# One step moved inside several side jobs of a hybrid encoder layer: turns, keys, logarithm rounds, buffers and stores

## The chip, the cores and the metric

The kernel runs on one core of one Trainium2 chip. The metric is the device time of one execution in microseconds, the median over several executions. Lower is better.

## The reference, cut to what matters

One layer of an encoder is applied to two groups of rows with the same weights: 1024 rows ("sample") and 256 rows ("prompt"), each 2048 wide, in float32. Everything between the two large products is done per head or per group of heads:

```python
hn = rms_norm(x, norm_g)
xbc, z_ssd, dt_raw, q, k, v, z_att, mq, z_mem = split_cols(hn @ w_in, IN_SIZES)
xbc = silu(centred_dwconv(xbc, conv_w, conv_b))            # 5 taps along the rows
dt = softplus(dt_raw + dt_bias); A = -exp(a_log)
y = ssd_scan(xs, dt[0], A[0], B, C) + reversed(ssd_scan(...)) + d_skip * xs
o_ssd = rms_norm(y * silu(z_ssd))                          # 16 heads of 64, chunks of 128 rows
o_att = window_attention(rms_norm(q), rms_norm(k), v, sink) * silu(z_att)
mk, mv = split_cols(rms_norm(mem) @ w_mem_kv)              # 256 memory rows for each group
pm = softmax(rms_norm(mq) @ rms_norm(mk).T / sqrt(128))    # 4 heads of 128
o_mem = (pm @ mv) * silu(z_mem)
return x + concat([o_ssd, o_att, o_mem]) @ w_out
```

The scan needs running sums of `dt * A` along a chunk (`acs`) and the logarithm of `dt`.

## The kernel before, in words

The 1280 rows make ten tiles of 128 (`NT`), in two groups of five. Tiles 0 to 7 are the sample, 8 and 9 the prompt. Every large product is taken in a split form: a float32 operand is cut into a high and a low part (ScalarE copies the high part, VectorE subtracts it, `wsplit`, L214 to L218), and three matmuls add up high times high, high times low and low times high.

The large products run as blocks, one behind the other, and TensorE does them in program order. `block_tok` (L244) computes 512 columns for up to five row tiles: for each of 16 slices of the inner dimension it loads 256 KB of weights on SyncE (L223), splits them, and issues 15 matmuls. `block_feat` does the same with the result turned. `block_pair` computes two halves at once with seven products in place of eight; 14 such blocks stand near the start and 8 at the end. When a tile of a block is complete, an eviction function takes it from the accumulator to SBUF and stores it to HBM: `ev_gate` (gates z0 and z1), `ev_raw` (queries q and mq), `ev_out` (the output) and others. In the last slice of a block the tiles finish one after the other.

An eviction's buffer comes from a ring. Rings `evt` and `evu` of the pool `ev` have two buffers each. Tiles with an odd number take `evt`, the others `evu`, so that tile 4 of a block takes the buffer that tile 0 had. The ring `ch` of the pool `rp` has four buffers (`CH`) and serves the loads that refill the rows (`fill_direct`, L185), the output's evictions and the sums near the end.

Everything that isn't a large product is a side job, written as a generator, whose parts between two `yield`s are its steps. Two lanes hold the queued jobs: lane 0 the keys (`k_prep`), the window attention (`attn`) and the memory attention (`mem_attn`), lane 1 the preparation of dt (`dt_prep`) and the scan (`ssd_up`, `ssd_down`). Behind each slice of a block, `pump` (L158) adds a rate to what is owed to each lane and runs as many steps, in turns between the lanes; the rates stand in `RATES` (2.25 and 2.5 steps a slice in the second query block, for instance). A job that ends takes one more step, so that a final `yield` is an empty step. `need` runs a lane's steps until a named job is done. The framework then gives each engine one order of instructions, by the order in the program and by its own estimate of when an operand is ready; `tc.high_priority` moves evictions and splits forward. On the chip, each engine goes through its order without overtaking.

The jobs that the change touches:

- `mem_attn(t)` (L773 to L870). Step 1 takes the query (fetched by the job before, `fetch_next`, L524), step 2 the sum of squares, step 3 the split of the query and the load of the gate, step 4 is empty, steps 5 and 6 are the scores of two heads each (`scores`: matmuls L811 to L813, maximum L815, exponentials L821 on ScalarE, the division L827 on VectorE). Steps 7 and 8 are empty, 9 and 10 turn the weights (`turn_`: GpSimd's clearing of one word L654, four transposes L647, copy L839 on ScalarE), 11 and 12 are the values (`values`: matmuls L850, product L853). Step 11 also fetches the next query, step 12 stores the result (L869). Step 13 is the empty end.
- `k_prep(t)` (L530 to L560). Step 3 splits the key, step 4 is empty, step 5 does four transposes (L554), two copies and the fetch of what comes next; step 6 is the empty end.
- `dt_prep(t0)` (L568 to L636), once for each group of five tiles. Step 1 is the softplus (L578 to L589), step 2 the product with A (`da`, L593), step 3 a first value of the logarithm (L596, L597), step 5 a triangular mask on GpSimd (`lower`, L602), step 7 the running sums on TensorE (`pacs`, L608 to L610), their copy on ScalarE, two rounds that refine the logarithm (an exponential L614 on ScalarE, then L616 to L620 on VectorE, a reciprocal among them) and the exponentials of the sums (L621, L622); step 8 turns the sums (`pact`) and stores them. Steps 4 and 6 are empty, step 9 is the empty end.
- `refill_o(grp, when)` (L1531). It is called behind each slice `k` of a block. At the slices named in `when` it first makes sure by `need` that a part of the layer's output is complete, and then queues four loads of that part (L188, one a slice) with their splits (L197 to L201), which follow two slices after the load. In the first output block it is called with `{1: 2, 5: 3}`: the scan's two halves.
- `ev_pair(u)` (L1232). It adds the seven products of one of the last 8 blocks into two row tiles `r0`, `r1` of 2 x 320 (adds on VectorE, L1240) and stores them: all of `r0` behind product 3 (L1256), one half of `r1` behind product 7 (L1259), the other behind product 4, the last (L1262). The products come in the order 1, 2, 6, 5, 3, 7, 4.

## Time and profile before

| what | value |
|---|---|
| median of 3 runs | 1772.34 us (1772.21 to 1774.35) |
| profiled execution | 1773.66 us, of which the span of the core is 1772.0 us |
| TensorE busy | 1762.2 us (99% of the span) |
| VectorE, ScalarE, GpSimd busy | 1246.0, 901.6, 555.6 us |
| data moved by DMA | 301.16 MB, mean 170 GB/s |
| granted TensorE clock | full in all 40 slices of the span |

The profile is of one execution. In the rows that follow, PE is TensorE's matmuls, PEld its weight loads, DVE is VectorE, ACT ScalarE, POOL GpSimd and SP SyncE; a "q" behind the name means the engine's queue, for instance a DMA that SyncE issues. `L827` is line 827 of the kernel. A row in order of time gives the start and the duration in us, engine, line, instruction, the tile written and the tiles read, the shape and how many; in square brackets stand the idle time of that engine just before and what ended it. A row in the list of waits gives the engine and line that waited, what it waited for, the total in us, the number of times and the longest. The end of a matmul is modelled, so starts are safer than ends.

### The profile page before, as it was taken

The numbers are of one execution on the slowest core, as the hardware profiler recorded it, in microseconds if no ns is written. First come the engines' busy times: TensorE is split into PE (matmuls) and PEld (weight loads), VectorE is DVE, ScalarE is ACT, GpSimd is POOL, SyncE is SP. The second block draws the span as 40 slices with busy tenths as digits, with TensorE's granted clock in tenths as the row PEclk, the third lists the DMA queues.
The fourth block names the chain that finished last, engine by engine and source line by source line (L and its number), as shares of the span: only waits on it lengthen the run. The fifth ranks groups of instructions, "written<-read, shape, count | busy, mean of one in ns | idle before, by whom it ended". The sixth has DMA issues, their size and how long they took to land. (4 is left out here: it accounts for less than half of the span.)

```text
span 1772.0 us, 31942 instructions
## 1 busy us (share of the span) xinstructions
PE 1762.2 (99%) x11044; PEld 1608.4 (91%) x11044; DVE 1246.0 (70%) x2351; ACT 901.6 (51%) x2010; POOL 555.6 (31%) x980
## 2 busy tenths in 40 slices
PE   9999999999999999999999999999999999999999
PEld 7889999999998999999889988888988888899999
DVE  5596788888868878878665676566776654766665
ACT  6555455554434756656454555544446533543332
POOL 0105899998810100001001000011110000058775
PEclk9999999999999999999999999999999999999999
DMA  9654444445446645454545645557777755744442
GB/s 308 189 182 130 136 151 146 144 140 169 124 140 209 197 134 151 140 153 122 186 121 173 201 149 161 172 161 249 225 246 226 257 188 148 218 142 148 145 144 77
DMA packets 208210, 301.16 MB, mean 170 GB/s; under 512 B 19568, under 2 KB 86192, under 8 KB 208048
## 3 DMA queue, kind: packets, MB, share of 16 engines
q1 hardware_dynamic: 207904, 299.06, 54.1%
q8 instruction: 87, 1.43, 0.3%
q14 instruction: 75, 0.61, 0.1%
q10 hardware_dynamic: 144, 0.06, 0.0%
HBM read 236.36 MB, written 62.69 MB: 169 GB/s over the span
## 5 line engine op out<-in xcount | busy, mean ns | idle before, releaser
L217 DVE TENSOR_TENSOR wl<-wraw,wh 128x512 fp32r<-128x512 f32 (+1 forms) x480 | 346.4, 724 | 238.4 <-ACT wh L216 225.4
L216 ACT ACTIVATE wh<-wraw 128x512 fp32r<-128x512 f32 (+1 forms) x480 | 292.2, 613 | 301.6 <-PE acc L270 154.6
L268 PE MATMUL acc<-wh,xH 128*128 128x512 f32 (+1 forms) x1088 | 418.1, 385 | 0.0
L270 PE MATMUL acc<-wh,xL 128*128 128x512 f32 (+1 forms) x1088 | 410.4, 377 | 0.0
L269 PE MATMUL acc<-wl,xH 128*128 128x512 f32 (+1 forms) x1088 | 409.5, 376 | 0.0
L270 PEld LDWEIGHTS acc<-wh,xL 128*128 128x128 f32 x1088 | 204.2, 188 | 37.0 <-issue 0.2
L268 PEld LDWEIGHTS acc<-wh,xH 128*128 128x128 f32 x1088 | 204.3, 188 | 36.5 <-issue 2.7
L269 PEld LDWEIGHTS acc<-wl,xH 128*128 128x128 f32 x1088 | 204.5, 188 | 35.0 <-issue 1.2
L303 PE MATMUL acc<-xH,wh 128*128 128x320 f32 x640 | 203.0, 317 | 0.0
L305 PE MATMUL acc<-xH,wl 128*128 128x320 f32 x640 | 198.8, 311 | 0.0
L304 PE MATMUL acc<-xL,wh 128*128 128x320 f32 x640 | 198.5, 310 | 0.0
L216 ACT ACTIVATE sh<-ws 128x384 fp32r<-128x384 f32 x176 | 91.4, 523 | 204.8 <-POOL ws L1284 111.2
L217 DVE TENSOR_TENSOR sl<-ws,sh 128x384 fp32r<-128x384 f32 x176 | 124.4, 710 | 98.3 <-ACT sh L216 96.0
L1284 POOL TENSOR_TENSOR ws<-wraw 128x128 f32<-128x128 f32 x176 | 113.8, 646 | 202.4 <-DMA wraw<-in_w_in_pairs_dram 90.5
L303 PEld LDWEIGHTS acc<-xH,wh 128*128 128x128 f32 x640 | 120.1, 188 | 2.9 <-issue 2.4
L304 PEld LDWEIGHTS acc<-xL,wh 128*128 128x128 f32 x640 | 120.2, 188 | 1.7 <-issue 1.4
L305 PEld LDWEIGHTS acc<-xH,wl 128*128 128x128 f32 x640 | 120.2, 188 | 1.0 <-issue 0.9
L1284 POOL TENSOR_TENSOR ws<-wraw,ws 128x128 f32<-128x128 f32 x176 | 116.5, 662 | 13.8
L1284 POOL TENSOR_TENSOR ws<-ws,wraw 128x128 f32<-128x128 f32 x176 | 118.2, 671 | 0.0
L1284 POOL TENSOR_TENSOR wraw<-wraw 128x128 f32<-128x128 f32 x176 | 111.5, 633 | 13.7
L654 POOL MEMSET lgw<- 128x1 f32 x40 | 4.2, 105 | 312.0 <-DVE lg L718 161.6
L377 DVE SCALAR_TENSOR_TENSOR c<-u,vec,c 128x638 f32<-128x638 f32 (+1 forms) x96 | 90.0, 939 | 1.1 <-ACT c L372 0.4
(442 smaller groups left out, 3931.1 us busy)
## 6 DMA issues: line engine op xcount, KB each, us to landing
wraw<-in_w_in_laid_dram SPq DMA_DIRECT2D x176, 256.0 KB, 2.9
wraw<-in_w_in_pairs_dram SPq DMA_DIRECT2D x112, 256.0 KB, 2.7
wraw<-in_w_out_laid_dram SPq DMA_DIRECT2D x64, 256.0 KB, 3.6
wraw<-in_w_out_pairs_dram SPq DMA_DIRECT2D x64, 256.0 KB, 2.7
rf<-ac SPq DMA_DIRECT2D x40, 256.0 KB, 4.0
rb<-ac SPq DMA_DIRECT2D x40, 256.0 KB, 4.7
wraw<-in_w_mem_laid_dram SPq DMA_DIRECT2D x32, 256.0 KB, 4.3
xst<-in_x_sample_dram SPq DMA_DIRECT2D x20, 256.0 KB, 5.3
```

The costliest lines, as they stand in the source:

```text
L216: a = A.activation(h, raw, AF.Copy)
L217: b = V.tensor_sub(l, raw, h.bitcast(F32))
L268: T.matmul(ps[t][:, :n], sh, h[:, :n], start=(k_ == 0), stop=False)
L269: T.matmul(ps[t][:, :n], sh, l[:, :n], start=False, stop=False)
L270: T.matmul(ps[t][:, :n], sl, h[:, :n], start=False, stop=(k_ == KT - 1))
L303: T.matmul(o, sh, cur["H", q][:, m, c], start=(k == 0), stop=False)
L304: T.matmul(o, sh, cur["L", q][:, m, c], start=False, stop=False)
L305: T.matmul(o, sl, cur["H", q][:, m, c], start=False, stop=(k == KT - 1))
L377: V.scalar_tensor_tensor(out=c[0], in0=u[:, k:k + n], scalar=cw[k], in1=c[0], op0=ALU.mult, op1=ALU.add)
L654: G.memset(w.bitcast(F32)[(slice(None),) + tuple(slice(n - 1, n) for n in shape)], 0.0)
L1284: G.tensor_tensor(out=o, in0=x, in1=y, op=op)
```

## The change

Six edits, each of which moves or splits something; no product is added or removed.

- `out_place` (new): evictions of tiles 3 and 4 in the second group's gate and query blocks (z0, z1, q, mq) take a buffer of the ring `ch`. All others stay.
- `k_prep`: the fetch stays in step 5, the transposes and copies go to step 6, in place of the empty end.
- `dt_prep`: the mask goes to step 2; the running sums go to step 5 with the exponentials of the sums and the first round; the second round is step 6; the rest of step 7 and step 8 stay.
- `mem_attn`: the turns go to steps 10 and 11, the values to 12 and 13; the fetch stays in step 11.
- `ev_pair`: the upper half of `r0` is stored behind product 2, so that behind product 3 only the lower half is left; the add of `w` to `r1` is done in two halves, behind products 6 and 5.
- `refill_o` with `sooner=1` and `{2: 2, 6: 3}` in the first output block: `need` stays at slices 1 and 5, the loads and splits go one slice later.

```diff
+    def out_place(i, base, name):
+        if i > 2 and base == 0 and name == "qs":
+            return fin.tile([P, 512], F32, tag="tH7" if i == 4 else "tL7", name=name)
+        if i > 2 and base:
+            return rp.tile([P, 640], F32, tag="ch", name=name, bufs=CH)[:, :512]
+        return ev.tile([P, 512], F32, tag="evt" if i % 2 else "evu", name=name)
...
     def ev_gate(c, base):
-            z = ev.tile([P, 512], F32, tag="evt" if i % 2 else "evu", name="zs")
+            z = out_place(i, base, "zs")
...
     def ev_raw(dst, base):
-            if base == 0 and i > 2:
-                z = fin.tile([P, 512], F32, tag="tH7" if i == 4 else "tL7", name="qs")
-            else:
-                z = ev.tile([P, 512], F32, tag="evt" if i % 2 else "evu", name="qs")
+            z = out_place(i, base, "qs")
...
     def k_prep(t):
         yield
         yield
+        fetch_next()
+        yield
         ps = psum("pk")
...
         A.activation(kL[:, :, c], hv(ps[:, 256:], 2), AF.Copy)
-        fetch_next()
-        yield
...
     def dt_prep(t0):
         V.tensor_mul(t5(da), dt_all[:, ts, :], aneg.unsqueeze(1).broadcast_to([P, 5, 32]))
+        lower = w2("lower")[:, :P]
+        G.affine_select(out=lower, in_=ones, compare_op=ALU.is_ge, fill=0.0, base=0,
+                        pattern=[[-1, P]], channel_multiplier=1)
         yield
...
-        yield
-        yield
-        lower = w2("lower")[:, :P]
-        G.affine_select(out=lower, in_=ones, compare_op=ALU.is_ge, fill=0.0, base=0,
-                        pattern=[[-1, P]], channel_multiplier=1)
         yield
         yield
         ps = psum("pacs")
...
         A.activation(ac[:, :320], ps[:, :320], AF.Copy)
+        A.activation(flat(eacs_all), ac[:, 0:160], AF.Exp)
+        A.activation(flat(cd_all), ac[:, 160:320], AF.Exp)
         for _ in range(2):
             A.activation(s, l, AF.Exp)
...
             V.scalar_tensor_tensor(out=l, in0=d, scalar=2.0, in1=l, op0=ALU.mult, op1=ALU.add)
-        A.activation(flat(eacs_all), ac[:, 0:160], AF.Exp)
-        A.activation(flat(cd_all), ac[:, 160:320], AF.Exp)
+            yield
         V.tensor_sub(wj, l, ac[:, 0:160])
...
     def mem_attn(t):
         scores(1)
-        yield
-        yield
-        yield
+        for _ in range(4):
+            yield
         turn_(0)
         yield
         turn_(1)
+        fetch_next()
         yield
         values(0)
-        fetch_next()
         yield
         values(1)
         S.dma_start(oT_d[1][grp][:, :, tc_], hv(oT, 4))
-        yield
...
     def ev_pair(u):
             elif p == 2:
                 add(r0[:, 0], ps, r0[:, 0])
+                S.dma_start(y_turned[rows_[0], :320], r0[:, 0])
             elif p == 6:
                 add(w[:, 0], ps, w[:, 0])
+                add(r1[:, 0], w[:, 0], r1[:, 0])
             elif p == 5:
                 add(w[:, 1], ps, w[:, 0])
                 add(r0[:, 1], w[:, 1], r0[:, 1])
-                add(r1, w, r1)
+                add(r1[:, 1], w[:, 1], r1[:, 1])
             elif p == 3:
                 add(r0[:, 1], ps, r0[:, 1])
-                S.dma_start(hv(y_turned[rows_[0], :], 2), r0)
+                S.dma_start(y_turned[rows_[0], 320:], r0[:, 1])
...
-    def refill_o(grp, when):
+    def refill_o(grp, when, sooner=0):
         def f(k):
+            if k + sooner in when:
+                need((attn, mem_attn, ssd_down, ssd_down)[when[k + sooner]], range(grp * 5, grp * 5 + 5))
             if k not in when:
                 return []
             q = when[k]
-            need((attn, mem_attn, ssd_down, ssd_down)[q], range(grp * 5, grp * 5 + 5))
...
-        tok("o", w_out_rows(c), ev_out(c * 512), None if c else refill_o(0, {1: 2, 5: 3}), grp=1)
+        tok("o", w_out_rows(c), ev_out(c * 512), None if c else refill_o(0, {2: 2, 6: 3}, sooner=1), grp=1)
```

## The prediction, on record before the run

> **What bounds the kernel now.** I read the page first, then the busy time by stage, then the list of who waited for whom on TensorE, then the instructions in order of time around each of those waits. Columns of the stage rows: microseconds from and to, length, then busy time and count of matmuls, weight loads, VectorE, ScalarE, GpSimd, then the granted clock.
>
> ```profile
> span 1772.0 us, 31942 instructions
> PE 1762.2 (99%) x11044; PEld 1608.4 (91%) x11044; DVE 1246.0 (70%) x2351; ACT 901.6 (51%) x2010; POOL 555.6 (31%) x980
> ...
> 0.00:490.00 490.00, 488.36 (x2973) 461.67 (x2974) 370.86 (x567) 256.13 (x499) 311.34 (x482) 1.00 0.53 165
> ...
> 812.00:946.00 134.00, 132.06 (x840) 117.95 (x839) 95.09 (x216) 74.53 (x196) 12.51 (x27) 1.00 0.52 158
> ...
> 1182.00:1312.00 130.00, 128.62 (x839) 112.22 (x839) 96.35 (x199) 60.32 (x145) 19.50 (x52) 1.00 0.71 223
> 1312.00:1500.00 188.00, 186.85 (x1001) 155.37 (x1000) 105.91 (x205) 88.33 (x206) 11.15 (x33) 1.00 0.67 212
> ...
> 1592.00:1772.00 180.00, 176.35 (x1202) 176.08 (x1200) 114.77 (x182) 65.45 (x117) 127.40 (x217) 1.00 0.42 128
> ```
>
> TensorE is idle for 1772.0 - 1762.2 = 9.8 us in all, at the full granted clock. 1.6 us of that lie in the first stage and 3.65 us in the last one, nearly all behind the last matmul. The three stages in the middle hold 1.94 + 1.38 + 1.15 = 4.5 us. So this change, which removes no matmul, can take about 4.5 us off the middle and a part of the tail. These are the waits:
>
> ```profile
> ...
> PE pst L937 <- ACT fh L952: 1.1, 1, 1.1
> PE pmt L647 <- DVE mpr L827: 1.1, 1, 1.1
> PE ppt L647 <- ACT pT L734: 1.0, 1, 1.0
> PE pmo L850 <- ACT mpT L839: 0.8, 1, 0.8
> PE pr L647 <- ACT so L1088: 0.4, 1, 0.4
> ...
> ```
>
> Every one is a single event (the two rows left out lie in the first and the last stage). The first four, 1.1 + 1.1 + 1.0 + 0.8 = 4.0 us, are what the edits touch.
>
> **Memory attention turned one step later.** The wait at 846 us:
>
> ```profile
> 845.87 0.62 DVE L827 TENSOR_SCALAR mpr<-mpr,mden 128x256 f32<-128x256 f32 x2
> 846.37 0.54 PE L647 MATMUL pmt<-identr,mprw 128*128 128x128 f32 x4 [1.06 <-DVE mpr L827]
> ...
> 848.54 1.05 PE L850 MATMUL pmo<-mpT,mv 128*128 128x128 f32 x8
> ```
>
> The second turn stands on TensorE before VectorE has divided the weights. The number of steps of one memory attention stays 13, because the empty end step is dropped; scores stay at steps 5 and 6, the turns go from 9 and 10 to 10 and 11, the values from 11 and 12 to 12 and 13, and the fetch of the next query stays in step 11. I call a step place the point behind each group of main matmuls where the lanes' steps are put. The next place here is that of the first values, at 848.54, 3.2 us behind the point where TensorE now begins to wait (846.37 - 1.06): minus 1.06 us. Nothing is late next there, as the values move a place on as well. With the turn go GpSimd's clearing of one word and ScalarE's copy, with the values VectorE's product and the store on SyncE; the fetch was ahead of that store before and stays so.
>
> A later turn has a price where three steps share a place, as in the third memory attention (steps 10, 11, 12 at 875 us). Now it holds turn 1, values 0, values 1; after, turn 0, turn 1, values 0. Its rows, with dt_prep's logarithm beside them:
>
> ```profile
> 874.92 0.46 PE L647 MATMUL pmt<-identr,mprw 128*128 128x128 f32 x4
> 875.91 0.34 ACT L614 ACTIVATE s<-l 128x160 f32<-128x160 f32 x1 [2.05 <-DVE l L620]
> ...
> 876.67 0.58 ACT L839 ACTIVATE mpT<-pmt 128x512 f32<-128x512 f32 x1
> 877.30 1.16 PE L850 MATMUL pmo<-mpT,mv 128*128 128x128 f32 x8 [0.79 <-ACT mpT L839]
> ```
>
> ScalarE stands 2.05 us before the exponential of the second logarithm round, and the copy of the turned weights, ready to go at 874.92 + 0.46 = 875.4, is queued behind it. In the change the two exponentials of the running sums go ahead of the rounds, each round gets a step of its own, and the sums come two steps sooner. I count minus 0.79 for this. In its place stands the new order: the values need a turn (0.46) and a copy (0.58), and beside the copy lie only another turn (0.46) and two transposes of dt_prep, half a turn, so some 0.3 us of the 1.04 since the turn's start stay open. An estimate of plus 0.3 us; the ends are 0 (main matmuls are put in between) and 0.79 (what the place costs now). Behind it are queued all main matmuls.
>
> **The sums of dt_prep two steps sooner.** Step counts again stay (9), but the matmuls that add up the decays go from step 7 to step 5, with ScalarE's copy of them and the two exponentials. At 2.5 steps a place the second dt_prep's steps fall as 1-2, 3-5, 6-7, 8-9, which fits the sums at 871 us (step 7) one place ahead of the turn at 875. So they move to the place of the second scores:
>
> ```profile
> 866.85 0.28 PE L813 MATMUL pms<-mkH,mql 128*128 128x256 f32 x1
> L593 DVE TENSOR_TENSOR e<-dt_all,aneg x2: 319/322/324, 537.1 to 868.6; 128x160 f32<-128x160 f32 x2
> L609 PE MATMUL pacs<-e,lower x4: 275/275/275, 544.4 to 871.0; 128*128 128x80 f32 x4
> ```
>
> Their operand is written on VectorE at 868.6 + 0.3 = 868.9. Put right behind the last score matmul at 866.9, TensorE would wait 2.0 us, with all main matmuls and ScalarE's copy of the sums behind it; put behind main matmuls of the next place, 0. I take 1.0, the size that misplaced steps have in this trace (0.8 to 1.1), and keep 0 and 2.0 as ends. The first dt_prep has no such price: its operand stands at 537.4, its sums run at 544.4, and two steps at 1.7 a place are one or two places of 3.45 us, so not before 537.5. The mask on GpSimd moves three steps forward; GpSimd is busy for 12.5 us of 134 in this stage, so it costs nothing.
>
> **Own places for the fourth and fifth eviction.** The last rows of the query block at 1227 us:
>
> ```profile
> 1227.20 0.60 ACT L341 ACTIVATE qs<-acc 128x512 f32<-128x512 f32 x1 [1.06 <-DMA mq<-qs]
> ...
> 1228.12 0.65 PE L647 MATMUL ppt<-identr,lgw 128*128 128x128 f32 x4 [0.95 <-ACT pT L734]
> DMA to landing us min/median/max: 2.2/3.6/5.4
> ```
>
> The fifth eviction takes the buffer of the first, whose store is still under way; ScalarE stands in front of it, the window attention's copy pT stands behind, TensorE behind that. With a buffer of the ring "ch", which no fill uses during those blocks, the wait of 1.06 goes, and with it TensorE's 0.95. [...]
>
> **Wait for the store ahead of the load.** The chain of waits around 1330 us:
>
> ```profile
> 1317.83 0.23 PE acc L270
> ...
> 1319.97 4.54 DMA oT<-so
> ...
> 1324.90 5.86 DMA chd<-oT
> 1331.52 0.62 ACT wh L216
> ...
> 1334.10 0.64 ACT fh L952
> 1334.78 0.50 PE pst L937
> ```
>
> SyncE waits for the last output to land, then loads it; ScalarE's first split of that load waits for it with a weight split queued behind, and the state's matmuls are late. The change finishes the scan one place earlier than it asks for the load. From place to place lie fifteen matmuls of 0.23, 3.45 us, and the steps, most of the 4.54; loads and splits both go one place on, so that the store has landed when the load's turn comes: minus 1.1 us. The later load brings the splits of a row block from five to four places ahead of its use, over 13 us: no cost.
>
> **Keys.** Their transposes go one step later and the fetch stays in its step. No row of TensorE's waits names them: 0, between minus 0.3 and plus 1.0, the size of one misplaced step.
>
> **The tail.** VectorE sets the end behind the last matmul:
>
> ```profile
> 1765.75 0.49 DVE L1240 TENSOR_TENSOR yu<-acc,yu 128x320 f32<-128x320 f32 x1 [0.39 <-PE acc L1318]
> 1766.27 1.23 DVE L1240 TENSOR_TENSOR yr<-yu,yr 128x320 f32<-128x320 f32 x2
> 1767.82 1.41 DVE L1240 TENSOR_TENSOR yr<-accm,yr 128x640 f32<-128x640 f32 x2
> L1240 DVE TENSOR_TENSOR yr<-yu,yr 128x320 f32<-128x320 f32 x8 | 4.0, 500 | 0.3
> ```
>
> One half of the 640-wide add moves into the idle 0.39 us ahead of 1765.75. It takes 0.50 and so delays the next add by 0.11; the pair of 1.23 becomes two adds of 0.50, 0.23 less. Together minus 0.12 us. 160 of the last 640 KB go out sooner, with one more issue on SyncE, which no engine waits for: an estimate of minus 0.1, between minus 0.3 and plus 0.1. [...]
>
> **Sum.** Minus 1.06 - 0.79 - 0.95 - 1.1 - 0.2, plus 0.3 + 1.0: minus 2.8 us. The profiled execution took 1773.66 us (span 1772.0 and 1.66 around it), so 1770.9 for it; the runs shown have a median of 1772.34, 1.3 lower, and I forecast 1769.5 for the median. About 0.2%, 3.5 us here, is what a measurement of this kernel can tell from no change: the lines are 1768.8 and 1775.9.
>
> **The rivals.**
>
> First, all four waits go and the sums of dt_prep find their operand ready, because main matmuls stand ahead of them: no plus at all, 1772.34 - 4.1 = 1768.2. For it speaks that TensorE meets late steps only five times between 490 and 1500 us, so most are placed well; against it the 2.0 us between 866.9 and 868.9. Chance 0.33.
>
> Second, the waits change their places and do not go: 2.0 us at the sums and 0.79 twice where turns and values share a place give back 3.6 of 4.1: 1771.8. For it speaks that all steps after scores shift and that VectorE, 71% busy in that stage, is late there whatever the order. Chance 0.20.
>
> Third, slower: SyncE holds the weights. The memory attention's store is issued in order, and where it waits, the next weight load waits too:
>
> ```profile
> 1389.77 0.33 SPq L223 DMA_DIRECT2D wraw<-in_w_out_laid_dram  x1
> 1396.66 0.53 SPq L869 DMA_DIRECT2D oT<-moT  x1
> 1398.44 0.40 SPq L223 DMA_DIRECT2D wraw<-in_w_out_laid_dram  x1
> 1412.18 0.63 ACT L216 ACTIVATE wh<-wraw 128x512 fp32r<-128x512 f32 x1 [1.59 <-PE acc L270]
> wraw<-in_w_out_laid_dram SPq DMA_DIRECT2D x64, 256.0 KB, 3.6
> ```
>
> After the change this store waits one place longer, 3.45 us and the steps, about 5 us. The weights that it holds back are needed 1412.18 - 1398.44 = 13.7 us after their issue and land in 3.6, so a margin of 10 us is left, 5 after the change. It decides only from 10 us on; a hold of 18 us would cost 8 us of TensorE and give 1772.34 - 2.8 + 8 = 1777.5. Chance 0.07.
>
> **How the numbers follow.** The forecast's own case has 0.40, with 1768.8 to 1771.3 around it. Faster by over 0.2% is the first rival, 0.33; slower the third, 0.07; within 0.2% the forecast and the second, 0.60. The range goes from 1767.0 (first rival, with the tail's and the keys' lower bounds and some 0.5 us of other waits) to 1772.8 (second rival with one more wait of 1.0).
>
> **What would show it.** In the changed kernel's list of TensorE's waits the rows for pmt, ppt, and pst should be gone, and no eviction should wait for its own store. The sums (pacs) should stand near 867 us; a wait of TensorE for L593's tile there is the 1.0 to 2.0 us that I count. ScalarE should not stand before the second logarithm round with a copy behind it. At the end, two stores of 160 KB should replace the one of 320 KB, and the last add should start about 0.1 us sooner against the last matmul. The prediction is wrong if TensorE's idle time in the middle stages stays near 4.5 us, or if a weight split waits for its load.

## The result, and the profile after

The changed kernel is slower: a median of 1776.50 us (7 runs, 1776.12 to 1781.02) against 1772.51 of the kernel before on the same chip (7 runs, 1771.51 to 1774.43), a ratio of 1.0026 with a 95% interval of 1.0016 to 1.0036. (A ratio, here and below, is estimated from all the runs; the quotient of the two medians differs from it by up to 0.0006.) The forecast was 1769.5 and the range ended at 1772.8. The profiled execution took 1776.12 us, its span 2.4 us more than that of before. From the page of the changed kernel, the span and the busy time:

```profile
span 1774.4 us, 31955 instructions
...
PE 1764.4 (99%) x11044; PEld 1609.0 (91%) x11044; DVE 1250.4 (70%) x2359; ACT 901.5 (51%) x2010; POOL 557.2 (31%) x980
```

The number of matmuls is unchanged, but TensorE is *busy* 2.2 us longer (1764.4 against 1762.2): the lost time is not all idle time. The stage rows (columns as in the prediction) say where:

```profile
490.00:812.00 322.00, 320.74 (x2255) 301.13 (x2254) 248.31 (x546) 180.52 (x438) 31.72 (x77) 1.00 0.51 157
812.00:946.00 134.00, 131.97 (x837) 117.57 (x837) 96.82 (x221) 76.59 (x203) 13.16 (x27) 1.00 0.53 158
...
1182.00:1312.00 130.00, 129.48 (x858) 113.05 (x854) 97.28 (x202) 60.16 (x145) 19.95 (x56) 1.00 0.73 233
1312.00:1500.00 188.00, 186.42 (x992) 154.69 (x992) 106.85 (x205) 87.02 (x204) 11.51 (x33) 0.99 0.66 207
```

The three middle stages hold 2.03 + 0.52 + 1.58 = 4.1 us of idle time, where before they held 4.5; 1.26 us in the stage from 490 us come on top, where before it was 0.07. And one number that was 1.00 everywhere is 0.99: the granted clock from 1312 us. TensorE's waits (total, times, longest):

```profile
PE pacs L611 <- DVE e L598: 1.9, 1, 1.9
PE pst L939 <- ACT fh L954: 1.4, 1, 1.4
...
PE pst L940 <- DVE fl L962: 0.7, 2, 0.4
PE acc L303 <- DVE zs L327: 0.7, 2, 0.4
PE pd L1124 <- DVE wl L217: 0.5, 1, 0.5
PE pacs L611 <- DVE w L604: 0.2, 1, 0.2
```

The rows for pmt and ppt are gone, as forecast, and so is the one for pmo. The row for pst is there still, and longer, with a second one for the low half fl: 0.22 us of that lie right behind the wait for fh, the other 0.44 at 575 us. New are the sums (pacs), the gates of the second stage (zs, at 588 us), and pd (at 1245 us).

**The sums.** In order of time, around 867 us of the changed kernel:

```profile
867.01 0.28 PE L817 MATMUL pms<-mkH,mql 128*128 128x256 f32 x1
...
869.22 0.32 DVE L598 TENSOR_TENSOR e<-dt_all,aneg 128x160 f32<-128x160 f32 x1
...
869.68 0.42 PE L611 MATMUL pacs<-e,upper 128*128 128x80 f32 x2 [1.93 <-DVE e L598]
```

Only two main matmuls lie between the last score and the sums. In this execution that is the upper end of the bound, 2.0, nearly to the digit; I had taken 1.0.

**The refill.** SyncE's stores and loads, ScalarE's splits and the state's matmuls, in order of time, first of the changed kernel:

```profile
1320.39 1.21 SPq L1091 DMA_DIRECT2D oT<-so  x2
...
1325.78 1.27 SPq L188 DMA_DIRECT2D chd<-oT  x3
...
1328.56 0.43 SPq L188 DMA_DIRECT2D chd<-oT  x1
...
1333.74 0.83 ACT L200 ACTIVATE xH<-chd,vec 128x640 fp32r<-128x640 f32 x1 [0.97 <-DMA chd<-oT]
1334.48 0.61 ACT L954 ACTIVATE fh<-xf 128x512 fp32r<-128x512 f32 x1
...
1335.14 0.50 PE L939 MATMUL pst<-fh,bth 128*128 128x512 f32 x1 [1.36 <-ACT fh L954]
1335.87 0.65 PE L940 MATMUL pst<-fl,bth 128*128 128x512 f32 x1 [0.22 <-DVE fl L962]
```

And the same place of the kernel before:

```profile
1324.53 1.75 SPq L188 DMA_DIRECT2D chd<-oT  x4
...
1334.10 0.63 ACT L952 ACTIVATE fh<-xf 128x512 fp32r<-128x512 f32 x1 [0.52 <-DVE xf L950]
...
1334.78 0.50 PE L937 MATMUL pst<-fh,bth 128*128 128x512 f32 x1 [1.09 <-ACT fh L952]
1335.12 0.39 PE L268 MATMUL acc<-wh,xH 128*128 128x512 f32 x1
1335.51 0.50 PE L938 MATMUL pst<-fl,bth 128*128 128x512 f32 x1
```

Two things differ. Before, the four loads go out together and fh waits last for xf of VectorE, which stands itself at the end of a chain from the load (its rows come below, with the reasons); after, the fourth goes out 2.8 us behind the first three, and its split, which waits for it, stands directly ahead of fh. And before, a main matmul lies between the state's product with fh and the one with the low half fl, of which TensorE waits the rest; after, nothing does, and TensorE waits for fl too: 0.73 us lie between the starts of the two products where a main matmul takes 0.23, so some 0.5 us are lost, of which the profile counts 0.22 as idle.

**The clock.** Matmuls, granted clock, DMA share and GB/s, microsecond by microsecond, and two rows of the chain that ended last:

```profile
1334.00:1335.00 1.00, 0.00 (x0) 1.00 1.04 399
1335.00:1336.00 1.00, 0.64 (x2) 1.00 1.06 395
1336.00:1337.00 1.00, 1.00 (x3) 0.53 1.09 363
1337.00:1338.00 1.00, 1.00 (x3) 0.50 0.67 244
1338.00:1339.00 1.00, 1.00 (x4) 0.50 0.93 205
1339.00:1340.00 1.00, 1.00 (x5) 0.76 0.83 147
```

```profile
1338.65 0.43 PE acc L269
...
1341.17 0.23 PE acc L269
```

Behind the wait for fh the granted clock falls to half for about 3.4 us (0.47 + 0.50 + 0.50 + 0.24 of a microsecond lost, 1.7 us in all), and a main matmul takes 0.43 in place of 0.23. None of it shows as idle.

**The balance** of the two profiled executions. Gone: pmt 1.06, ppt 0.95, pmo 0.5 (by the starts of the rows, 0.3 of the 0.79 is left), pr 0.4, and 0.35 at the end (span end less last matmul's start: 3.6 after, 4.0 before). Come: pacs 1.9 + 0.2, the clock 1.7, pst 0.3 + 0.7, zs 0.7, pd 0.5. That is minus 3.3 and plus 6.0: plus 2.7, against a measured 2.4.

### The profile page after: what moved, and what is told of

It reads as the page before. It is cut to its first block, busy times and chain, and to the rows that moved or that the text cites. A ratio compares the mean times of both kernels' runs of the same rounds, so it can differ in the third digit from the quotient of the medians.

```text
span 1774.4 us, 31955 instructions
## 1 busy us (share of the span) xinstructions
PE 1764.4 (99%) x11044; PEld 1609.0 (91%) x11044; DVE 1250.4 (70%) x2359; ACT 901.5 (51%) x2010; POOL 557.2 (31%) x980
## 4 chain that ended last, share of the span: by engine, by line
PE 95%; DVE 3%; DMA 1%; issue 0%; ACT 0%; POOL 0%; SPq 0%; ACTq 0%; DVEq 0%
PE acc L268 12%; PE acc L270 12%; PE acc L269 12%; PE acc L1322 7%; PE acc L1320 7%; PE acc L1321 7%; PE acc L303 5%; PE acc L305 5%; PE acc L304 5%; PE accm L1320 3%; PE accm L1321 3%; PE accm L1322 3%; PE po L748 1%; PE pmo L854 1%; PE py L1016 1%; PE ppt L651 1%
```

## The experiments

Each kernel was timed with the kernel before on the same chip, 8 to 12 runs of it and 21 to 33 of that. The last column counts runs whose granted clock, as a mean over the run, was 0.999 or less: 3.4 us at half clock are 0.001 of a run.

| kernel | median us | before | ratio [95%] | clock under 1 |
|---|---|---|---|---|
| sums alone | 1774.55 | 1772.33 | 1.0011 [1.0002, 1.0020] | 2 of 11 |
| refill alone | 1773.10 | 1772.33 | 1.0009 [1.0000, 1.0018] | 4 of 11 |
| keys alone | 1772.17 | 1772.33 | 1.0001 [0.9992, 1.0010] | 1 of 11 |
| turns alone | 1772.16 | 1772.33 | 1.0001 [0.9992, 1.0010] | 0 of 11 |
| own places alone | 1772.26 | 1772.53 | 0.9998 [0.9989, 1.0007] | 0 of 11 |
| changed, dt step as before | 1773.66 | 1771.77 | 1.0013 [1.0004, 1.0022] | 8 of 11 |
| changed, refill as before | 1774.09 | 1771.77 | 1.0017 [1.0008, 1.0027] | 2 of 11 |
| changed, both as before | 1770.81 | 1771.77 | 0.9996 [0.9988, 1.0005] | 1 of 11 |
| changed, sums a step later | 1772.99 | 1771.77 | 1.0010 [1.0001, 1.0018] | 4 of 11 |
| that, refill as before | 1772.42 | 1772.53 | 1.0003 [0.9994, 1.0011] | 0 of 11 |
| that, refill a part sooner | 1776.25 | 1772.53 | 1.0019 [1.0010, 1.0028] | 5 of 11 |
| changed, wait filled | 1776.47 | 1772.53 | 1.0020 [1.0009, 1.0031] | 2 of 8 |
| both as before, first load later | 1772.88 | 1772.80 | 1.0000 [0.9992, 1.0009] | 4 of 12 |
| both as before, second load later | 1771.78 | 1772.80 | 0.9990 [0.9982, 0.9999] | 0 of 11 |
| before, fh made late | 1772.09 | 1772.80 | 0.9990 [0.9981, 0.9998] | 0 of 11 |
| dt step as before, fl a step apart | 1773.16 | 1772.11 | 1.0004 [0.9995, 1.0013] | 1 of 11 |
| dt step as before, fh twice first | 1774.08 | 1772.11 | 1.0005 [0.9996, 1.0013] | 8 of 11 |

### One part of the change at a time

The kernel before with the lines of `dt_prep` from the diff, and nothing else:

> Only the dt_prep edit, on the kernel before. Theory (the sums stand on TensorE two steps too soon): TensorE waits about 1.9 us for L593's tile at the second dt_prep and 0.2 us at the first, and the 0.8 us before the values at 877 us goes, so 1.0 to 1.5 us slower than before. Rival (the wait comes from the turns that were moved into the same stretch): without them no wait at the sums, and 0.5 to 0.8 us faster. If the logarithm rounds load VectorE and ScalarE at another place, the z1 gate's evictions at 588 us make TensorE wait here too (0.7 us).

Measured: ratio 1.0011. From its list of TensorE's waits:

```profile
PE pacs L606 <- DVE w L599: 1.1, 1, 1.1
```

The wait came, at the second dt_prep (868 us), shorter than the 1.9 that was expected, and the kernel is slower by 0.0002 to 0.0020 of the time: the dt step alone costs. Then the lines of `refill_o` and its call alone:

> Only the refill edit (loads and splits one slice later). Theory (the split that waits for its load now stands right in front of the state's split on ScalarE): the wait before the state's matmuls at 1335 us grows from 1.1 to 1.5 us or more, and if TensorE is idle there long enough the granted clock drops to half for 3.4 us as in the changed kernel, 1.7 us more; together 1.0 to 3.0 us slower, clock 0.999. Rival (the edit does what it is for and the longer wait comes from the turns that now share that place): the 1.1 us goes, 0.8 to 1.2 us faster, clock 1.000.

Measured: 1.0009. The wait did not go (0.9 and 0.2 in its profile), so the prediction's term of minus 1.1, here the rival, falls: its 0.9994 lies outside the interval. The longer wait of the theory, 1.5 or more, is not in that profile either, which is of the quickest of the eleven runs (1770.19). Four of eleven runs show a clock of 0.999, with a mean of 1775.1 against 1772.4 for the other seven. Then the lines of `k_prep` alone:

> Only the key edit (transposes in the last step, fetch before them). Theory (ScalarE's copy of the turned keys waits for VectorE in front of the gate's evictions): TensorE waits at the end of the z1 block near 588 us, 0.7 to 1.2 us slower than before. Rival (that wait comes from dt_prep's moved rounds): within 0.3 us of before.

Measured: 1.0001, as the rival had it. Its profiled execution is of use for another reason:

```profile
PE pst L937 <- ACT fh L952: 0.8, 1, 0.8
PE pr L647 <- ACT so L1088: 0.5, 1, 0.5
PE pmt L647 <- DVE mpr L827: 0.4, 1, 0.4
```

No line of the turns, the sums or the query block's evictions differs here from the kernel before, and yet ppt's 1.0 and pmo's 0.8 are not in the list, and pmt's 1.06 is 0.4. For pmt this can be followed from execution to execution. In the profiles of the sums alone, the refill alone, the keys alone and the kernel before with a late fh (told of below), the instructions of TensorE, VectorE and ScalarE stand in the same order in the 8 us ahead of this place as in the kernel before, and the wait that was 1.06 there is 0.25, 0.46, 0.39 and 0.25. The row of the keys alone:

```profile
845.31 0.53 PE L647 MATMUL pmt<-identr,mprw 128*128 128x128 f32 x4 [0.39 <-DVE mpr L827]
```

With ppt it is the same: in the keys alone the order is that of the kernel before, but the fifth eviction does not wait for the first one's store and ppt has no wait; in the sums alone ppt waits 1.0 again. So the size of these waits belongs to the execution that I had read, not to the kernel. The turns alone (the lines of `mem_attn`) and the own places alone (`out_place` and its two calls) then bring what this suggests:

> Only the memory attention edit. Theory: the wait of 1.06 us for the divided weights at 846 us goes; at 875 us the values wait for their turn's copy much as before (0.3 to 0.8 us): 0.7 to 1.5 us faster. Rival (the later turns fall on the scan's state matmuls at 1335 us and hold ScalarE there): the wait at 1335 us grows by 0.5 us or more, the clock drops to half once, and the edit is 0.5 to 2 us slower.

> The kernel before with the own places of the evictions alone. Theory A (waits seen in one execution are not there in each: the runs of the turns alone and of the keys alone measured nothing): the wait of ppt for pT (1.0) is gone in the profile, the median is within 0.5 of the kernel before's. Rival B (my term of the prediction): 0.95 faster than before.

Measured: 1.0001 and 0.9998. In each the wait that it aims at is gone from the profile, and by the intervals the time is the same within 1.1 parts in a thousand. Of the turns neither expectation came true, the gain of 0.7 or more no more than the loss; of the places theory A did.

### One part undone at a time

The expectations of this group count the steps of `dt_prep` from zero: their fourth, fifth and sixth are the text's steps 5, 6 and 7. First the changed kernel with all lines of `dt_prep` as before:

> The changed kernel with the dt step's own lines as before (the sums back at their sixth step, both logarithm rounds in one step, lower mask in its own step); all else as changed. Theory A (the sums' wait at 867 costs about 2 us, the refill the rest): the 1.9 us wait of pacs for e and the 0.2 us one for w are gone, the median falls by about 2 from the changed kernel's 1776.5, to 1774 to 1775; the half clock behind the state's wait at 1334 stays, so the granted clock is 0.999 in most runs. The wait of the gates for zs at 588 (0.7 in two) goes if it came from the dt step beside the keys. Rival B (the time comes from all parts together, each undone edit gives back only a small share): 1776 or above.

Measured: 1.0013, and 8 of 11 runs at 0.999 or less, means of 1774.6 for these and 1772.3 for the other three. Then the changed kernel with `refill_o(0, {1: 2, 5: 3})`:

> The changed kernel with the refill's two loads at their old places (1 and 5, need at the same place); all else as changed. Theory A (refill's later first load puts its rounding in front of the state's high half on ScalarE, and TensorE's near-idle 2 us there lets its clock fall to half for 3.4 us): the granted clock reads 1.0 in nearly all runs, the wait of pst for fh is back near 0.9 to 1.2 with no second wait for fl, no stretch at 1336 to 1340 below 0.9 of the clock; the median falls by 1.5 to 2.5 from the changed kernel's, to 1774 to 1775. Rival B (the half clock comes from the timing of the whole and not from the refill): clock still 0.999 in most runs, 1776 or above.

Measured: 1.0017, 2 of 11. Theory A holds for both: undoing one gives back 0.0013, undoing the other 0.0009, and the clock comes back with the refill. Its profiled execution was its quickest run, 1771.8. It has no wait for fh and 0.7 for fl, other than expected, and for the sums a wait of only 0.5, so this wait, too, differs from execution to execution. Both undone:

> The changed kernel with both the dt step and the refill as before: own places, keys, memory attention's turns, and the store and sum at the end as changed. Theory A (the two carry the whole loss): 1771.5 to 1772.5, that is the kernel before's time or up to 0.8 under it, with the waits pmt, ppt and pacs absent. My sum in the prediction for these parts (own places -0.95, turns -1.06, tail -0.2) would give 1770.1; rival B (neighbours' waits come up in place of those removed): 1772.3 or more, with the clock at 1.0.

Measured: 0.9996 [0.9988, 1.0005]. So the two edits together carry the whole loss, 0.0030 of the time or some 5 us. What is left is not slower than the kernel before, and not measurably faster. Its list holds a wait of 1.0 for pmo and one of 1.7 for fh, and none for the gates' zs, which is 0.3 with the dt step as before and 0.6 with the refill as before, and in neither the sums alone nor the keys alone; what makes that wait was not tried.

Is it the *place* of the sums, or the split rounds? The changed kernel with the sums one step later:

```diff
+        yield
         ps = psum("pacs")
...
-        for _ in range(2):
+        for rnd in range(2):
...
-            yield
+            if rnd == 0:
+                yield
```

> The changed kernel with the sums one step later (their fifth step instead of the fourth; the second logarithm round then shares the step of the differences); all else as changed. Theory A (pacs waits because its place lies 2 us before its operand is ready): pacs's wait at 868 is gone, since one step is over 3 us of matmuls, and the median falls by about 2 from the changed kernel's, to 1774 to 1775. Rival B (it is the second round and the exponentials on ScalarE and VectorE that cost, wherever the sums lie): the wait goes and the time stays at 1776 or above, with new waits of 0.5 or more for ScalarE between 870 and 890.

Measured: 1.0010. No wait for pacs in the list; its rows in order of time are the proof of the place:

```profile
866.84 0.28 PE L819 MATMUL pms<-mkH,mql 128*128 128x256 f32 x1
...
869.04 0.32 DVE L598 TENSOR_TENSOR e<-dt_all,aneg 128x160 f32<-128x160 f32 x1
...
870.38 0.34 PE L612 MATMUL pacs<-e,upper 128*128 128x80 f32 x2
```

The operand comes when it came in the changed kernel, 2.2 us behind the last score; the sums now stand 3.5 us behind it. From 1.0026 to 1.0010 are 0.0016 or 2.8 us for one step, as theory A expected, though the two intervals touch. With the refill as before on top of it:

> The changed kernel with the refill as before and the sums one step later (their fifth step); own places, keys, turns, store, exponentials ahead and the split rounds as changed. Theory A (refill and the sums' place carry the whole loss, the rest of the dt step costs nothing): 1770 to 1771.5, the kernel before's less 0.5 to 2, clock 1.0 in nearly all runs, no wait of pacs, pmt, ppt. Rival B (the split rounds cost by themselves): above the kernel before's by 0.5 or more.

Measured: 1.0003, no run under full clock, no wait for pacs, pmt or ppt. The split rounds and early exponentials neither cost nor bring anything that can be seen, and the gain that theory A still expected did not come: waits of 2.1 for fh and 1.1 for pmo are in its list.

### The refill and the clock

If a load that comes late is the trouble, a sooner one should help. The kernel just told of with `{0: 2, 4: 3}`:

> The kernel of e12 with the refill's two loads one part sooner than before (0 and 4) in place of one part later. Theory A (on ScalarE the rounding of the refill stands in front of the state's high half and waits for its load; the sooner the load, the sooner fh): the wait of pst for fh at about 1332 falls from 0.9 to 1.7 to under 0.5, and the median is 0.5 to 1.5 under e12's. Rival B (SyncE's queue or the vector engine's xf sets fh): the wait stays at 0.9 or more, same time as e12 or slower.

Measured: 1.0019; theory A falls. Its waits of pst became one of 0.8 for mm and one of 1.4 for fl, both of VectorE, and the clock fell in the profile as well (columns as before):

```profile
1330.00:1332.00 2.00, 0.62 (x3) 1.00 0.78 193
1332.00:1334.00 2.00, 2.00 (x7) 0.72 0.93 333
1334.00:1336.00 2.00, 2.00 (x6) 0.50 0.87 288
1336.00:1338.00 2.00, 2.00 (x12) 0.93 0.87 252
```

So the old place is better than either neighbour. The profiles name different waits for that: with the load later, its split holds up fh on ScalarE; with the load sooner, VectorE is behind. Next, work put into the wait of the changed kernel:

```diff
                 ps = psum("pst")
+                if t == NS and g == 0:
+                    for _ in range(12):
+                        T.matmul(ps[:, :256], bth[:, 0, :], bth.rearrange("p a b -> p (a b)"), start=True, stop=True)
                 into(ps, g, fh, fl)
```

> The changed kernel, with twelve matmuls of 256 columns on bth into the state's PSUM tile ahead of its first real matmul of token block 8, which overwrites them: about 1.4 us of TensorE work inside the wait of 1.4 to 2.9 us for fh at 1334. Theory A (the near-idle there lets the granted clock fall to half for 3.4 us in most runs): the granted clock is 1.0 in nearly all runs, no stretch at 1335 to 1341 below 0.9, and the median is 0.5 to 1.5 under the changed kernel's 1776.5, though the wait itself stays. Rival B (the clock falls for another reason): 0.999 in most runs as in the changed kernel, time as there or up to 1 slower.

Measured: the clock is 1.0 in 6 of 8 runs where the changed kernel had it in 1 of 7, which speaks for the near-idle stretch as what releases the drop. The time is no better (1.0020 against 1.0026, the intervals overlap): in the profile the twelve matmuls take 1.67 us and the waits behind them still 0.5 + 0.2, so what the clock gave back, the filling took. Which of the two loads it is, in the changed kernel with both parts as before:

```diff
-refill_o(0, {1: 2, 5: 3})
+refill_o(0, {2: 2, 5: 3}, late=(2,))   # first load alone; its need() stays at 1
+refill_o(0, {1: 2, 6: 3}, late=(3,))   # second load alone; its need() stays at 5
```

> The kernel of e11 (sums and refill as before) with the refill's first load alone one part later, its need at the old place. Theory A (all of the refill's cost is at the state's wait at 1330 to 1334, where the first load's rounding stands in front of fh): about e9's time, 1773.2 to 1774.2, with the granted clock at 0.999 in half or more of the runs and the wait of pst for fh over 1. Rival B (the second load, four parts on, carries half or more): under 1772.2 and the clock at 1.0 in nearly all.

> The kernel of e11 with the refill's second load alone one part later, its need at the old place. Theory A: e11's time, 1770.3 to 1771.5, clock 1.0 in nearly all runs. Rival B (the second load carries half or more of it): 1772.2 or more.

Measured: the second load alone costs nothing (0.9990, clock 1.0 in all 11). The first alone has the lower clock in 4 of 12 runs, with a mean of 1776.1 against 1772.2 for the other eight. Its median is less slow than expected, 1.0000 where both loads moved gave 1.0013; the intervals touch, and whether the second load adds something beside the first stays open. Last, a late fh without any refill moved:

```diff
-                parted[0] = A.activation(fh, xf, AF.Copy).ins
+                for _ in range(3 if t == NS and g == 0 else 1):
+                    parted[0] = A.activation(fh, xf, AF.Copy).ins
```

> The kernel before with the rounding that makes fh done three times over in token block 8's first half (the same values): ScalarE gives fh out about 1.05 later (two more at 0.52), all else as before. Theory A (a longer wait there drops the granted clock for 3.4 us, a loss of about 1.7 each time, whatever made the wait longer): the clock is 0.999 in a third or more of the runs, and these are 1.5 to 2.3 slower than the others; the median is 1 to 2.5 above the kernel before's. Rival B (the clock falls only with the refill's moved transfers): 1.0 in nearly all runs, and the median is 0.5 to 1.1 above.

Measured: 0.9990, clock 1.0 in all runs. This one tells nothing about what a longer wait does to the clock: eight main matmuls came to lie between the turn and pst, so the wait was 1.1 us, as in the kernel before. It does show how far a ratio goes by itself: a kernel that only does more work reads 0.1% faster, with an interval that leaves out 1. The 0.9990 of the second load is to be read by that measure, and I do not call it a gain. The differences of 0.0007 to 0.0021 between two kernels, from which the costs of the sums and of the refill are read, are not much larger; what speaks for them is that they have one sign in every pair.

Taken together, in the five kernels with the first load a part later (changed, refill alone, dt step as before, sums a step later, first load later) 26 of 52 runs have a clock under 1. In the nine with the first load as before it is 6 of 99, and in the kernel before itself 13 of 146. In the profiles of the five, fl's product follows fh's with no main matmul between, 0.72 us from start to start; in the profiles of the nine, main matmuls lie between. That the clock falls at this place in the other runs, too, is not shown: of these profiles only the changed kernel's has the drop. Nor is one drop, 1.7 us, the whole difference of the runs that have it: where the two groups were set apart above, they lie 2.2 to 3.9 us from each other. The last two kernels go at that stretch. Both are the changed kernel with the dt step as before (8 of 11, 1.0013):

```diff
-                into(ps, g, fh, fl)
+                if t == NS and g == 0:
+                    T.matmul(ps, bth[:, g, :], fh, start=True, stop=False)
+                    T.matmul(ps, btl[:, g, :], fh, start=False, stop=False)
+                    yield        # in the first of the two kernels only
+                    T.matmul(ps, bth[:, g, :], fl, start=False, stop=True)
+                else:
+                    into(ps, g, fh, fl)
```

> The changed kernel with the dt step as before (8 of 11 runs under full clock, ratio 1.0013), and in token block 8's first half the state's product with the low half fl put a step behind the two with fh, so that a group of main matmuls lies between. Theory A (the refill's move costs because no main matmuls are left between fh's and fl's product, so that the near-idle stretch goes on for 0.7 us more and drops the clock): no wait of pst for fl, clock 1.0 in two thirds of the runs or more, and a ratio of 1.0005 or less, that is 1 to 3 us less. Rival B (the wait for fh alone drops the clock): the wait for fl is gone, the clock is still under 1 in half the runs or more, ratio 1.0010 or more.

> The same base, with the three products in the order fh with bth, fh with btl, fl with bth in that half: one matmul of 0.23 us fills a part of the wait of 0.49 for fl, nothing else moves. Theory A: the near-idle stretch is 0.2 us shorter; the clock is under 1 in somewhat fewer runs than 8 of 11, ratio 1.0008 to 1.0013. Rival B: no change in either, 7 to 9 of 11 and 1.0011 to 1.0015.

Measured: 1 of 11 and 8 of 11. The first did not come out as it was meant: no main matmul lies between its products either, but the added step moved the neighbours, and the wait for fh is short. From the order of time of the first and then of the second:

```profile
1332.39 0.50 PE L973 MATMUL pst<-fh,bth 128*128 128x512 f32 x1 [0.48 <-ACT fh L955]
1332.72 0.40 PE L974 MATMUL pst<-fh,btl 128*128 128x512 f32 x1
1333.12 0.51 PE L976 MATMUL pst<-fl,bth 128*128 128x512 f32 x1
```

```profile
1333.68 0.50 PE L973 MATMUL pst<-fh,bth 128*128 128x512 f32 x1 [1.75 <-ACT fh L955]
```

The refill is moved in both. Where the profile has a wait of 0.5 us the clock stays in 10 of 11 runs, where it has 1.8 us it falls in 8 of 11 (as rival B expected, though not in the profiled execution). This speaks against the moved transfers themselves and for the near-idle stretch that they leave. Without the stretch 1.0013 becomes 1.0004; the intervals overlap, so a gain of time is indicated and not shown. The second kernel's ratio is 1.0005 and the quotient of its medians 1.0011, so what its order of products is worth stays open.

The length of one wait does not decide it, though. The profiled execution with the dt step as before waited longest of all and kept its clock (columns as before):

```profile
1330.00:1332.00 2.00, 0.40 (x5) 1.00 0.95 320
1332.00:1334.00 2.00, 0.52 (x2) 1.00 1.05 398
1334.00:1336.00 2.00, 2.00 (x9) 1.00 0.93 323
```

TensorE is busy for 0.92 us of 4 there, and for 0.62 of 2 in the kernel with the refill sooner and 0.64 of 2 in the changed kernel (1334 to 1336 us), where the clock fell. Nor is it the moved load alone that leaves such a stretch: with the sums a step later and the refill as before TensorE was busy for 0.02 us of the 2 from 1332.6 us, and the clock was full in that execution as in all eleven runs. So a near-idle stretch is not enough for the drop, and what decides is not shown.

## Why the prediction was wrong

**The waits to be removed (minus 1.06, 0.79, 0.95).** The mechanisms were right: the rows are gone. The sizes were not, and this is the first step that failed: "The first four, 1.1 + 1.1 + 1.0 + 0.8 = 4.0 us, are what the edits touch". I took a list of one execution as the kernel's constant. That execution took 1773.66 us, 1.3 over the median, which I noted and only subtracted; I did not conclude that some of the 4.0 us were that very excess. In other executions of the same instructions pmt's wait was 0.25 to 0.46. Turns alone, own places alone and the kernel with both (and keys and tail) brought 1.0001, 0.9998 and 0.9996, where the terms asked for 0.9994, 0.9995 and 0.9988. The terms lie inside or at the lower ends of the intervals, so a part of them may be there; what the profiles show is that these waits come and go with nothing changed at their places.

**The sums (plus 1.0, between 0 and 2.0).** The mechanism and the place were named, the term was too small. The wait was 1.9 in the profiled execution of the changed kernel, and 1.6, 1.1 and 0.5 in three others with the sums in this place (wait filled, sums alone, refill as before), so 1.0 lies inside what the profiles show. The times ask for more. By the five pairs of kernels with and without the sums in this place (the sums alone, two with the dt step as before, two with the sums a step later) 0.0011 to 0.0021 of the time depend on it, 1.9 to 3.7 us, each difference uncertain by some 0.0013 by the intervals of its two ratios; how what goes beyond the wait comes about is not settled. "I take 1.0, the size that misplaced steps have in this trace" took its size from other places, where the row nearest to the question gave 2.0. Also wrong was "The first dt_prep has no such price": there the sums stand at 537 us in the changed kernel and wait 0.2 us for VectorE.

**The refill (minus 1.1).** The step that failed is "so that the store has landed when the load's turn comes". SyncE issues the loads 5.4 us behind the store's issue (1320.39 and 1325.78), and such a store takes 4.9 us in the median to land in this stretch, so the place that was gained did not put the load behind a store long landed. ScalarE waits for the loads as before: 1.1 and 0.97 us at 1329.9 and 1333.7, where it was 0.3 and 1.3 before, and the second of these waits now stands directly ahead of fh. That the load sets the state's matmuls was read rightly: in the chain that ended last of the kernel before, the load is followed by the weight split wh on ScalarE (1331.52), then by VectorE up to xf, then by fh (1334.10):

```profile
1332.17 0.69 DVE wl L217
1332.86 0.60 DVE xs L932
1333.46 0.61 DVE xf L950
```

What is late next when the load comes in time was not asked; in the one kernel with the load sooner it is VectorE's fl, 1.4 us. Instead of minus 1.1 the move costs 0.0007 to 0.0017 by the three pairs with and without it, 1.2 to 3.0 us, and 0.0009 alone. One part of that is the half clock, 1.7 us in the changed kernel's profile; one is the wait for fl, some 0.5; how the rest comes is not settled.

**Turn 0, turn 1 and values in one place (plus 0.3).** Right in size, and in part by luck. By the starts of the rows 0.31 us lie between the end of the main matmul ahead (877.70, 0.23 long) and the values (878.24), of which the profile counts 0.07 as idle. But from the turn to the values it took 1.37 us where 1.04 were reckoned, and the main matmul that filled 0.23 of that stood only in the lower end of the estimate, not in its 0.3.

**Keys (0) and tail (minus 0.2).** Keys alone measured 1.0001. The tail's 0.2 is the 0.12 of the adds and the 0.1 of the stores together. At the end the last pair of adds starts 0.50 us ahead of the last matmul, and 0.22 before the change (1767.82 and 1768.04):

```profile
1770.29 1.41 DVE L1242 TENSOR_TENSOR yr<-accm,yr 128x640 f32<-128x640 f32 x2
...
1770.79 0.31 PE L1322 MATMUL accm<-rH,wl 128*128 128x320 f32 x1
```

So 0.28 us sooner where 0.1 were forecast, and the span's end 0.35 us nearer to the last matmul; too small to be seen in the times.

**The rivals.** The first failed by the 2.0 us that it named against itself. The second, waits that change their places, is what happened in the profile (4.1 us idle for 4.5), and with it came the prediction's own sign of being wrong, idle time in the middle stages near 4.5; but its price, 1771.8, lacked the clock and the length of the new waits. The third, SyncE holding the weights, did not occur: from 812 to 1500 us, where that store is, no weight split of the changed kernel waits for its load, and SyncE stands for moT 4.6 us at most. That the result could be slower because the edits themselves misplace work, I priced only as an end of the range, never as a case with a chance.

## What to carry to other kernels

A wait in one profiled execution is a sample. Before it goes into a sum, see whether another execution of the same instructions has it; what a kernel with 4.5 us of scattered idle time can win is what recurs. When an operand's time and a new place's time are both in the trace, their difference is a better first price than a typical size between the two ends. And before a step is moved to wait less for one operand, look for the next one that comes late at the same place: here the last split of a load and VectorE's xf were ready 0.5 us apart in the kernel before (1333.6 and 1334.1) and 1.2 us apart in the changed one (1334.6 and 1333.4), and a move in either direction only changed what came last.

## What the runs showed of the hardware

In two profiled executions the granted clock fell to half for about 3.4 us behind a stretch in which TensorE was nearly idle for only about 2 us: in the changed kernel (busy for 0.54 us from 1333.9 to 1335.9) and with the refill a part sooner (0.62 us from 1330 to 1332). In each that is a loss of 1.7 us that no row shows as idle. The wait for the sums in the changed kernel's execution, 1.9 us at 867, had no such effect, nor had 2.9 us with the dt step as before, nor 2 us with 0.02 us of work with the sums a step later and the refill as before. So one profile cannot say whether a given wait is followed by such a drop; a mean clock under 1 showed in 26 of the 52 runs of the kernels with the first load moved later. The drop is found in the clock column of a narrow window, or by main matmuls of 0.43 us among those of 0.23.

Waits of 0.25 to 1.1 us came from the same instructions in the same order, in five executions (the transposes into pmt at 846 us), and the runs of the kernel before spread over 1769.7 to 1777.6 us in five series.
